# Row maxima of a 64 MB array: a short first load, the last two rows in four pieces, and merges behind them

## The chip, the cores and the metric

The kernel runs on one core of a Trainium2 chip. The metric is the device time of one execution in microseconds; lower is better. Beside it there is a profile of one execution: a page, and a trace that can be asked for timelines, waits and DMA issues.

## The reference

```python
x = np.random.randn(32, 512, 1024).astype(np.float32)

def reference(x):
    return np.max(x, axis=-1).astype(np.float32)
```

So 16384 rows of 1024 numbers are read, 67.1 MB, and one number a row is written, 64 KB.

## The kernel before, in words

The 16384 rows are spread over 128 partitions, 128 rows each. In the rest of the text "a row" means one row in every partition: 1024 elements for VectorE, 0.5 MB for the DMA engines. There are 128 of them, I in the code. `BLOCKS` cuts them into loads: a first block of 112 rows in ten loads (numbers 0 to 9, of 15, 15, 15, 14, 12, 11, 9, 8, 7 and 6 rows) and a second block of 16 rows, of which seven loads (numbers 10 to 16, of 4, 3, 2, 2, 1, 1 and 1 rows) take 14 and the last two rows come in pieces. The loads go into `ring`, a buffer of 46 rows, one behind the other; where a load does not fit any more it begins at the front again. All loads and pieces are issued by SyncE (SP), in order, L185 and L204 to L207. A load is issued when the reductions that read its place are done. SyncE's DMAs use eight semaphores in turn, so that each one also waits until the DMA eight places before it has landed.

Most of the work is on VectorE: one `reduce_max` for each load (helper `maximum`, L168), from the ring into `res`, which has one column a row. VectorE can't take all rows at the pace at which they arrive, so some columns of some rows go another way. `SHARED` names them: `9: (4, 4)` says that of load 9 the last 4 rows give their first 4 blocks of 128 columns away. `turn` (L125) transposes these blocks on TensorE into PSUM with the identity `ident` (L135), ScalarE copies them into SBUF (L141), and GpSimd (POOL) takes the maximum over the partitions (`partition_all_reduce`, L143), which is now the maximum over 128 columns of each row. `back` (L154) transposes a line of these maxima back into a column of a small PSUM tile, `fetched` (L161). VectorE reduces the other columns of these rows into the same tile, and `merge` (L170) reduces the tile over its blocks into `res`. In all 38 blocks of 128 columns go this way, in seven calls of `turn`.

The order on each engine is written out: `in_turn` chains the instructions of an engine in the order in which the program makes them. `TENSOR` lists the calls of `turn` and `back`, and `MERGE` says behind which load's reduction a merge stands.

The last two rows, seen as one line of 2048 columns in each partition, come in three pieces: the first 689 columns, the next 671, which end row one and begin row two, and the last 688. The second lies in `res` behind the place of the first one's maximum (column `AT - 1`), so that one reduction over two halves of 336 takes that maximum in, and gives both the first row's result and a maximum for the second row, at `MID - 1`, which the last reduction, of 689 columns, takes in (L212 to L217). Two merges stand between these two reductions.

The results leave by DMAs that ScalarE issues: the first block's 112 columns in three stores of 48, 48 and 32 partitions, behind the reduction of the first piece (L221), and the last 16 columns when everything is done (L223).

Of the kernel before, what the change touches and what calls it, by code (L numbers as in the profile page):

```python
# [8 lines left out]
F32 = mybir.dt.float32  # L9
# [1 line left out]


BLOCKS = [
    [15, 15, 15, 14, 12, 11, 9, 8, 7, 6],
    [4, 3, 2, 2, 1, 1, 1],
]
RING = 46


SHARED = {7: (2, 3), 9: (4, 4), 11: (3, 3), 13: (2, 3), 16: (1, 1)}  # L20


TENSOR = [
    ("turn", 7, 0), ("back", 7, 0), ("turn", 9, 0), ("turn", 9, 1),
    ("back", 9, 0), ("turn", 11, 0), ("turn", 11, 1), ("back", 9, 1),
    ("turn", 13, 0), ("back", 11, 0), ("back", 11, 1), ("turn", 16, 0),
    ("back", 13, 0), ("back", 16, 0),
]

MERGE = {8: (7,), 12: (9,), 15: (11,), 18: (13, 16)}  # L30
NOSYNC = mybir.DependencyInfo(mybir.DependencyClass.NoSync, mybir.DependencyReason.DATA)
SYNC = mybir.DependencyInfo(mybir.DependencyClass.Sync, mybir.DependencyReason.DATA)

# [1 line left out]
@with_exitstack  # L35
def kernel(
    ctx: ExitStack,
    tc: tile.TileContext,
    x: bass.AP,
    out: bass.AP,  # L40
):
    nc = tc.nc
    P = 128
    X = mybir.AxisListType.X
    ALU = mybir.AluOpType

    xf = x.flatten_outer_dims()
    N, D = xf.shape
    H = D // 2
    C = D // P  # L50
    I = N // P
    of = out.flatten_outer_dims()

    once = ctx.enter_context(tc.tile_pool(name="once", bufs=1))
    turned = ctx.enter_context(tc.tile_pool(name="turned", bufs=2))
    allr = ctx.enter_context(tc.tile_pool(name="allr", bufs=2))
    psum = ctx.enter_context(tc.tile_pool(name="psum", bufs=2, space=bass.MemoryType.PSUM))
    psmall = ctx.enter_context(tc.tile_pool(name="psmall", bufs=4, space=bass.MemoryType.PSUM))
    ring = once.tile([P, RING, D], F32)

    W = 336
    K = W - 1
    AT = I + 16
    MID = AT + K + W + 17
    res = once.tile([P, MID + D - W], F32)

    latest = {}

    def in_turn(engine, inst):

        if engine in latest:
            tc.add_manual_dep(inst.ins, latest[engine].ins.name, NOSYNC, reason="in turn")
        latest[engine] = inst
        return inst

    ident = once.tile([P, P], F32)  # L80
    colno = once.tile([P, P], F32)
    rowno = once.tile([P, 32], F32)
    in_turn("DVE", nc.vector.memset(ident, 1.0))  # L83
    in_turn("DVE", nc.vector.memset(rowno, 0.0))  # L84
    in_turn("DVE", nc.vector.tensor_tensor_scan(  # L85
        out=colno, data0=ident, data1=ident, initial=-1.0, op0=ALU.add, op1=ALU.mult))
    in_turn("DVE", nc.vector.transpose(out=rowno, in_=colno[:, :32]))  # L87
    for q in range(1, P // 32):
        part = rowno[q * 32:(q + 1) * 32, 0:1]
        in_turn("DVE", nc.vector.tensor_scalar(  # L90
            out=part, in0=part, scalar1=float(q * 32), scalar2=None, op0=ALU.add))
    in_turn("DVE", nc.vector.tensor_scalar(  # L92
        out=ident, in0=colno, scalar1=rowno[:, 0:1], scalar2=None, op0=ALU.is_equal))

    loads = []
    first = at = 0
    views = []
    for sizes in BLOCKS:
        S = sum(sizes) + 2 * (sizes is BLOCKS[-1])
        xb = xf[first * P:(first + S) * P, :].rearrange("(p i) d -> p i d", p=P)  # L100
        dst = bass.AP(tensor=of.tensor, offset=of.offset + first * P, ap=[[S, P], [1, S]])
        views.append((dst, res[:, first:first + S]))
        b = 0
        for n in sizes:
            if at + n > RING:
                at = 0
            loads.append((at, n, xb[:, b:b + n, :], first + b))
            at += n
            b += n
        first += S  # L110
    assert first == I

    def chunks(j):
        m, parts = SHARED[j]
        per = max(1, C // parts)
        return [(r, min(per, m - r)) for r in range(0, m, per)]

    def rows(j):
        start, n, _, _ = loads[j]
        return ring[:, start:start + n, :]  # L120

    tops = {}
    backs = {}

    def turn(j, c):  # L125


        m, parts = SHARED[j]
        r, q = chunks(j)[c]
        W = q * parts * P  # L130
        ps = psum.tile([P, D], F32)
        for i in range(q):
            for c0 in range(parts):
                k = i * parts + c0
                in_turn("PE", nc.tensor.transpose(  # L135
                    out=ps[:, k * P:(k + 1) * P],
                    in_=rows(j)[:, loads[j][1] - m + r + i, c0 * P:(c0 + 1) * P],
                    identity=ident,
                ))
        sb = turned.tile([P, D], F32)  # L140
        in_turn("ACT", nc.scalar.copy(out=sb[:, :W], in_=ps[:, :W]))  # L141
        top = allr.tile([P, D], F32)
        in_turn("POOL", nc.gpsimd.partition_all_reduce(  # L143
            top[:, :W], sb[:, :W], P, bass_isa.ReduceOp.max))
        tops[j, c] = top

    def share(j):
        m, parts = SHARED[j]
        if j not in backs:
            fetched = psmall.tile([P, parts + (parts < C), m], F32)  # L150
            backs[j] = fetched
        return backs[j]

    def back(j, c):  # L154

        m, parts = SHARED[j]
        r, q = chunks(j)[c]
        for i in range(q):
            for c0 in range(parts):
                k = i * parts + c0  # L160
                in_turn("PE", nc.tensor.transpose(  # L161
                    out=share(j)[:, c0, r + i:r + i + 1],
                    in_=tops[j, c][0:1, k * P:(k + 1) * P],
                    identity=ident[0:1, 0:1],
                ))

    def maximum(out, in_):
        return in_turn("DVE", nc.vector.reduce_max(out=out, in_=in_, axis=X))  # L168

    def merge(j):  # L170
        for i in MERGE.get(j, ()):
            _, k, _, c0 = loads[i]
            q, _ = SHARED[i]
            maximum(res[:, c0 + k - q:c0 + k], share(i).rearrange("p k m -> p m k"))


    issued = done = 0
    todo = list(TENSOR)
    for j in range(len(loads)):
        while issued < len(loads) and issued < j + 3:  # L180
            start, n, src, _ = loads[issued]
            held = any(s < start + n and start < s + k for s, k, _, _ in loads[j:issued])
            if held:
                break
            nc.sync.dma_start(out=rows(issued), in_=src)  # L185
            issued += 1
        while todo and todo[0][1] < (j if todo[0][0] == "back" else issued):
            what, i, c = todo.pop(0)
            (turn if what == "turn" else back)(i, c)
        _, n, _, col = loads[j]  # L190
        m, parts = SHARED.get(j, (0, 0))
        if n > m:
            maximum(res[:, col:col + n - m], rows(j)[:, :n - m, :])
        if m and parts < C:
            maximum(share(j)[:, parts, :], rows(j)[:, n - m:, parts * P:])
        merge(j)
    for what, i, c in todo:
        assert what == "back"
        back(i, c)

    if at + 1 > RING:
        at = 0
    piece = ring[:, at, :D - K]
    nc.sync.dma_start(out=piece, in_=xb[:, S - 2, :D - K])  # L204
    pair = xb[:, S - 2:, :].rearrange("p i d -> p (i d)")
    nc.sync.dma_start(out=res[:, AT:AT + K + W], in_=pair[:, D - K:D + W])
    nc.sync.dma_start(out=res[:, MID:], in_=pair[:, D + W:])  # L207
    latest_row = maximum(res[:, AT - 1:AT], piece)
    merge(len(loads))


    maximum(  # L212
        bass.AP(tensor=res.tensor, offset=res.offset + I - 2,
                ap=[list(res.ap[0]), [MID - 1 - (I - 2), 2]]),
        res[:, AT - 1:AT + K + W].rearrange("p (r k) -> p r k", r=2))
    merge(len(loads) + 1)
    maximum(res[:, I - 1:I], res[:, MID - 1:])  # L217


    for p, q in ((0, 48), (48, 96), (96, P)):  # L220
        store = nc.scalar.dma_start(out=views[0][0][p:q], in_=views[0][1][p:q])  # L221
        tc.add_manual_dep(store.ins, latest_row.ins.name, SYNC, reason="behind the loads")
    nc.scalar.dma_start(out=views[1][0], in_=views[1][1])  # L223


# [1 line left out]
_INS = ['x']  # L227
# [26 lines left out]
```

## Time and profile before

| | |
|---|---|
| time, median of 4 runs | 164.1 us (164.05 to 164.21) |
| the profiled execution | 164.21 us, of which the profile's span is 162.4 |
| VectorE (DVE) busy | 135.4 us, 83% of the span |
| TensorE (PE), ScalarE (ACT), POOL busy | 14.0, 6.4 and 16.2 us |
| DMA | 67.18 MB, mean 414 GB/s over the span |
| chain that ended last | DVE 57%, DMA 36%, issue 5% |
| `res<-ring` reductions, 15 of them | 124.1 us, idle before them 23.8, all for loads |

The span begins with the first instruction of the program and ends with its last one; the device time has 1.8 us more around it. The chain is followed back from the last instruction, at each step to what released it. In timelines a row has the start, the duration, the engine and line, the operation with output and inputs, and in brackets how long the engine was idle before and what ended that; rows marked x2 or more join instructions of one kind, and the starts and durations of neighbours can overlap a little, since VectorE begins an instruction before the one ahead of it has left its pipeline.

### The profile page before, as it was taken

To read this page: it belongs to the slowest core of one execution; us is meant where nothing else is said; L and a number is where in the kernel's file an instruction comes from. 1 tells how busy PE (TensorE), PEld (TensorE's weight loads), DVE (VectorE), ACT (ScalarE), POOL (GpSimd) and SP (SyncE) were. 2 spreads that over 40 slices of the span, in tenths; PEclk is the share of its full clock that TensorE was granted. 3 is DMA by queue.
4 is the path that set the end of the run, shared out by engine and by line. 5 is a ranking of instruction groups with operands and counts; after the bars stand their busy time and mean duration, and the time that the engine had idled before them with its cause. 6 is when DMAs were issued, how large, how long until landed. Compare 5 with 4: busy or idle time off the path is not lost.

```text
span 162.4 us, 305 instructions
## 1 busy us (share of the span) xinstructions
PE 14.0 (9%) x76; PEld 12.0 (7%) x76; DVE 135.4 (83%) x35; ACT 6.4 (4%) x8; POOL 16.2 (10%) x11
## 2 busy tenths in 40 slices
PE   0000000000000000000000000000003010736540
PEld 0000000000000000000000000000002010725440
DVE  3000069995999779998999999999999999999994
ACT  3000000000000000000000000000001000222020
POOL 0000000000000000000000000000000500095970
DMA  7998899979999799999998998999999999999990
GB/s 242 484 484 378 348 484 484 484 333 393 484 484 469 314 395 452 452 452 387 508 460 371 422 466 373 436 427 443 476 395 445 438 409 408 428 420 416 410 372 18
DMA packets 3200, 67.18 MB, mean 414 GB/s; under 512 B 640, under 2 KB 640, under 8 KB 1408
## 3 DMA queue, kind: packets, MB, share of 16 engines
q1 hardware_dynamic: 2880, 67.11, 96.7%
q10 hardware_dynamic: 320, 0.07, 0.2%
HBM read 67.11 MB, written 0.07 MB: 414 GB/s over the span
## 4 chain that ended last, share of the span: by engine, by line
DVE 57%; DMA 36%; issue 5%; DVEq 0%
DVE res L168 52%; DMA ring<-in_x_dram 36%; DVE fetched L168 5%; DVEq L249 0%
## 5 line engine op out<-in xcount | busy, mean ns | idle before, releaser
L168 DVE TENSOR_REDUCE res<-ring 128x15 f32<-128x15360 f32 (+10 forms) x15 | 124.1, 8302 | 23.8 <-DMA ring<-in_x_dram 23.8
L143 POOL PARTITION_ALL_REDUCE top<-sb x7 | 16.0, 2332 | 141.9 <-ACT sb L141 141.9
L135 PE MATMUL ps<-ident,ring 128*128 128x128 f32 x38 | 9.3, 423 | 134.0 <-DMA ring<-in_x_dram 134.0
L135 PEld LDWEIGHTS ps<-ident,ring 128*128 128x128 f32 x38 | 7.5, 222 | 134.2 <-issue 127.9
L141 ACT COPY sb<-ps 128x768 f32<-128x768 f32 (+3 forms) x7 | 5.1, 739 | 150.3 <-PE ps L135 150.3
L168 DVE TENSOR_REDUCE fetched<-ring 128x2 f32<-128x1280 f32 (+3 forms) x5 | 8.5, 1700 | 0.0
L161 PE MATMUL fetched<-ident,top 1*128 1x1 f32 x38 | 4.8, 243 | 10.8 <-DVE fetched L168 7.3
L161 PEld LDWEIGHTS fetched<-ident,top 1*128 1x128 f32 x38 | 4.5, 212 | 12.5 <-issue 8.0
L168 DVE TENSOR_REDUCE res<-res 128x2 f32<-128x672 f32 (+1 forms) x2 | 1.7, 858 | 0.0
L141 ACT ACT_TABLE_LOAD x1 | 1.3, 1283 | 0.7 <-PEq L238 0.7
L83 DVE MEMSET ident<- 128x128 f32 x1 | 0.2, 165 | 0.8 <-PEq L238 0.8
L168 DVE TENSOR_REDUCE res<-fetched 128x2 f32<-128x8 f32 (+3 forms) x5 | 0.7, 158 | 0.0
L90 DVE TENSOR_SCALAR rowno<-rowno 32x1 f32<-32x1 f32 x3 | 0.4, 146 | 0.1
L85 DVE TENSOR_TENSOR_SCAN colno<-ident 128x128 f32<-128x128 f32 x1 | 0.4, 425 | 0.0
L92 DVE TENSOR_SCALAR ident<-colno,rowno 128x128 f32<-128x128 f32 x1 | 0.3, 285 | 0.0
L87 DVE STREAM_TRANSPOSE rowno<-colno 128x32 f32<-128x32 f32 x1 | 0.2, 211 | 0.0
L238 POOL MEMSET const-float32-0.0<- 128x1 f32 x1 | 0.1, 99 | 0.2 <-issue 0.2
L238 POOL MEMSET const-bfloat16-1.0<- 128x1 bf16 x1 | 0.1, 103 | 0.0
L238 POOL MEMSET const-uint8-127<- 128x1 uint8 x1 | 0.1, 102 | 0.0
L238 POOL MEMSET const-float32-1.0<- 128x1 f32 x1 | 0.1, 99 | 0.0
L84 DVE MEMSET rowno<- 128x32 f32 x1 | 0.1, 85 | 0.0
## 6 DMA issues: line engine op xcount, KB each, us to landing
ring<-in_x_dram SPq DMA_DIRECT2D x3, 7680.0 KB, 38.5
ring<-in_x_dram SPq DMA_DIRECT2D x1, 7168.0 KB, 37.0
ring<-in_x_dram SPq DMA_DIRECT2D x1, 6144.0 KB, 33.4
ring<-in_x_dram SPq DMA_DIRECT2D x1, 5632.0 KB, 28.6
ring<-in_x_dram SPq DMA_DIRECT2D x1, 4608.0 KB, 39.1
ring<-in_x_dram SPq DMA_DIRECT2D x1, 4096.0 KB, 33.4
ring<-in_x_dram SPq DMA_DIRECT2D x1, 3584.0 KB, 29.0
ring<-in_x_dram SPq DMA_DIRECT2D x1, 3072.0 KB, 35.9
```

The source lines that it names most:

```text
L83: in_turn("DVE", nc.vector.memset(ident, 1.0))
L84: in_turn("DVE", nc.vector.memset(rowno, 0.0))
L85: in_turn("DVE", nc.vector.tensor_tensor_scan(out=colno, data0=ident, data1=ident, initial=-1.0, op0=ALU.add, op1=ALU.mult))
L87: in_turn("DVE", nc.vector.transpose(out=rowno, in_=colno[:, :32]))
L90: in_turn("DVE", nc.vector.tensor_scalar(out=part, in0=part, scalar1=float(q * 32), scalar2=None, op0=ALU.add))
L92: in_turn("DVE", nc.vector.tensor_scalar(out=ident, in0=colno, scalar1=rowno[:, 0:1], scalar2=None, op0=ALU.is_equal))
L135: in_turn("PE", nc.tensor.transpose(out=ps[:, k * P:(k + 1) * P], in_=rows(j)[:, loads[j][1] - m + r + i, c0 * P:(c0 + 1) * P], identity=i ...
L141: in_turn("ACT", nc.scalar.copy(out=sb[:, :W], in_=ps[:, :W]))
L143: in_turn("POOL", nc.gpsimd.partition_all_reduce(top[:, :W], sb[:, :W], P, bass_isa.ReduceOp.max))
L161: in_turn("PE", nc.tensor.transpose(out=share(j)[:, c0, r + i:r + i + 1], in_=tops[j, c][0:1, k * P:(k + 1) * P], identity=ident[0:1, 0:1],))
L168: return in_turn("DVE", nc.vector.reduce_max(out=out, in_=in_, axis=X))
L238: nc = _bacc.Bacc("TRN2", target_bir_lowering=False, num_devices=1)
```

## The change

The first block is cut into eleven loads, of 2, 13, 13, 15, 14, 11, 11, 10, 8, 8 and 7 rows, numbers 0 to 10; the second block's loads keep their sizes and are numbers 11 to 17. With the pieces there are 22 loads. The ring has 47 rows, and `res` is its first 128 columns instead of a tile of its own.

The shared rows are others: 3, 2 and 1 rows of loads 10, 12 and 14, six blocks each, and one row of load 17, two blocks; 38 blocks as before, in seven turns (`t0` to `t6`), one row each.

The last two rows are cut at columns 604 and 568 and come in the order 604 of row one, 568 of row two, 420 of row one, 456 of row two. A second piece lies behind one free column, into which the reduction of the same row's first piece writes its maximum; so the second reduction reads 421 or 457 columns and gives the row's result. All four reductions (`f0` to `f3`) have one input row.

The order is one list, `PLAN`: `d` is the reduction of a load's own rows, `p` that of a shared row's other columns, `t` and `b` are `turn` and `back`, `m` a merge, `f` a piece. On VectorE the tail reads: d15, d16, m12, p17, f0, f1, f2, m14, f3, m17. Loads are issued as early as the plan's readers allow. The first block's results leave in one store instead of three, behind `f0`.

```diff
 BLOCKS = [
-    [15, 15, 15, 14, 12, 11, 9, 8, 7, 6],
+    [2, 13, 13, 15, 14, 11, 11, 10, 8, 8, 7],
     [4, 3, 2, 2, 1, 1, 1],
 ]
-RING = 46
-SHARED = {7: (2, 3), 9: (4, 4), 11: (3, 3), 13: (2, 3), 16: (1, 1)}
-TENSOR = [
-    ("turn", 7, 0), ("back", 7, 0), ("turn", 9, 0), ("turn", 9, 1),
-    ("back", 9, 0), ("turn", 11, 0), ("turn", 11, 1), ("back", 9, 1),
-    ("turn", 13, 0), ("back", 11, 0), ("back", 11, 1), ("turn", 16, 0),
-    ("back", 13, 0), ("back", 16, 0),
-]
-MERGE = {8: (7,), 12: (9,), 15: (11,), 18: (13, 16)}
+RING = 47
+SHARED = {10: (3, 6), 12: (2, 6), 14: (1, 6), 17: (1, 2)}
+PIECES = [(604, 420), (568, 456)]
+PLAN = """
+    d0 d1 d2 d3 d4 d5 d6 d7 d8 d9 t0 d10 t1 t2 p10 d11 b0 b1 t3 d12 t4 p12 d13 b2 m10 t5 d14
+    p14 d15 b3 b4 d16 m12 p17 t6 f0 b5 f1 f2 b6 m14 f3 m17
+""".split()
...
-    ring = once.tile([P, RING, D], F32)
-    W = 336
-    K = W - 1
-    AT = I + 16
-    MID = AT + K + W + 17
-    res = once.tile([P, MID + D - W], F32)
+    ring = once.tile([P, I + RING * D], F32)
+    res = ring[:, :I]
...
+    at = at if at + last + 1 <= RING else 0
+    pieces = []
+    tail = []
+    room = I + at * D
+    for q in range(len(PIECES[0])):
+        for r, widths in enumerate(PIECES):
+            c, w = sum(widths[:q]), widths[q]
+            room = -(-(room + 1) // 16) * 16
+            pieces.append((ring[:, room:room + w], xb[:, S - last + r, c:c + w]))
+            if q:
+                tail[-last] = (ring[:, room - 1:room], tail[-last][1])
+            tail.append((res[:, I - last + r:I - last + r + 1],
+                         ring[:, room - (q > 0):room + w]))
+            room += w
...
-    piece = ring[:, at, :D - K]
-    nc.sync.dma_start(out=piece, in_=xb[:, S - 2, :D - K])
-    pair = xb[:, S - 2:, :].rearrange("p i d -> p (i d)")
-    nc.sync.dma_start(out=res[:, AT:AT + K + W], in_=pair[:, D - K:D + W])
-    nc.sync.dma_start(out=res[:, MID:], in_=pair[:, D + W:])
-    latest_row = maximum(res[:, AT - 1:AT], piece)
-    merge(len(loads))
-    maximum(
-        bass.AP(tensor=res.tensor, offset=res.offset + I - 2,
-                ap=[list(res.ap[0]), [MID - 1 - (I - 2), 2]]),
-        res[:, AT - 1:AT + K + W].rearrange("p (r k) -> p r k", r=2))
-    merge(len(loads) + 1)
-    maximum(res[:, I - 1:I], res[:, MID - 1:])
-    for p, q in ((0, 48), (48, 96), (96, P)):
-        store = nc.scalar.dma_start(out=views[0][0][p:q], in_=views[0][1][p:q])
-        tc.add_manual_dep(store.ins, latest_row.ins.name, SYNC, reason="behind the loads")
-    nc.scalar.dma_start(out=views[1][0], in_=views[1][1])
+    def issue():
+        nonlocal issued
+        while issued < len(loads):
+            start, n, src, _ = loads[issued]
+            if any(readers[j] and s < start + n and start < s + k
+                   for j, (s, k, _, _) in enumerate(loads[:issued])):
+                return
+            load = nc.sync.dma_start(out=rows(issued), in_=src)
+            issued += 1
+        if any(readers[j] and s < at + last + 1 and at < s + k for j, (s, k, _, _) in enumerate(loads)):
+            return
+        while pieces:
+            nc.sync.dma_start(out=pieces[0][0], in_=pieces[0][1])
+            pieces.pop(0)
+
+    for step in PLAN:
+        issue()
+        kind, k = step[0], int(step[1:])
+        if kind in "dp":
+            (direct if kind == "d" else partial)(k)
+            readers[k] -= 1
+        elif kind == "t":
+            turn(k)
+            readers[chunks[k][0]] -= 1
+        elif kind == "b":
+            back(k)
+        elif kind == "m":
+            merge(k)
+        else:
+            inst = maximum(*tail[k])
+            if behind is None:
+                behind = inst
+
+    for dst, src in views[:-1]:
+        store = nc.scalar.dma_start(out=dst, in_=src)
+        tc.add_manual_dep(store.ins, behind.ins.name, SYNC, reason="behind the loads")
+    nc.scalar.dma_start(out=views[-1][0], in_=views[-1][1])
```

## The prediction

> **What bounds the kernel now.** I read first the page's strip of 40 slices, then the chain that ended last in order of time, then VectorE's and SyncE's timelines, and last the DMA issues. The strip:
>
> ```profile
> DVE  3000069995999779998999999999999999999994
> DMA  7998899979999799999998998999999999999990
> ```
>
> Each digit is a busy tenth of 4.06 us. The DMA engines are busy from the first slice to the last but one; VectorE (DVE) has nothing to do before slice 6 and no gap from slice 19 on. Both end together, so there are two limits within a fraction of a microsecond of each other. The chain in order of time (start, length) says where VectorE hangs on a landing:
>
> ```profile
> 0.72 20.79 DMA ring<-in_x_dram
> ...
> 21.54 16.16 DVE res L168
> ...
> 74.75 55.86 DVE res L168 x5
> ```
>
> VectorE starts at 21.54, when load 0 (15 rows) has landed; from load 3 (14 rows, landed at 74.73 by the same chain) to the end it never stops. Its timeline shows the pace and the end:
>
> ```profile
> 39.67 16.15 DVE L168 TENSOR_REDUCE res<-ring 128x15 f32<-128x15360 f32 x1 [1.98 <-DMA ring<-in_x_dram]
> 57.81 16.16 DVE L168 TENSOR_REDUCE res<-ring 128x15 f32<-128x15360 f32 x1 [1.98 <-DMA ring<-in_x_dram]
> 74.75 55.86 DVE L168 TENSOR_REDUCE res<-ring 128x14 f32<-128x14336 f32 x5 [0.79 <-DMA ring<-in_x_dram]
> 130.53 1.48 DVE L168 TENSOR_REDUCE fetched<-ring 128x2 f32<-128x1280 f32 x1
> 131.92 7.61 DVE L168 TENSOR_REDUCE res<-ring 128x7 f32<-128x7168 f32 x1
> 139.45 0.16 DVE L168 TENSOR_REDUCE res<-fetched 128x2 f32<-128x8 f32 x1
> ...
> 157.46 0.86 DVE L168 TENSOR_REDUCE res<-ring 128x1 f32<-128x689 f32 x1
> 158.36 0.85 DVE L168 TENSOR_REDUCE res<-res 128x2 f32<-128x672 f32 x1
> 159.13 0.22 DVE L168 TENSOR_REDUCE res<-fetched 128x2 f32<-128x8 f32 x2
> 159.27 0.86 DVE L168 TENSOR_REDUCE res<-res 128x1 f32<-128x689 f32 x1
> ```
>
> From start to start, five reductions of 52 rows take 130.53 - 74.75 = 55.78 us and one of 7 rows takes 7.53. Two equations give 1.0665 us a row and 0.065 an instruction. The last reduction ends at 160.13.
>
> The stream's pace is in SyncE's timeline, whose late issues wait for the landing of the load eight places before (they take over its semaphore):
>
> ```profile
> 131.75 0.33 SPq L185 DMA_DIRECT2D ring<-in_x_dram  x1
> 139.06 0.33 SPq L204 DMA_DIRECT2D ring<-in_x_dram  x1
> 143.95 0.33 SPq L206 DMA_DIRECT2D res<-in_x_dram  x1
> 147.64 0.33 SPq L207 DMA_DIRECT2D res<-in_x_dram  x1
> ```
>
> Of the DMA issues (KB, us from issue to landing) I use two:
>
> ```profile
> res<-in_x_dram SPq DMA_DIRECT2D x1, 344.0 KB, 11.4
> out_dram<-res ACTq DMA_DIRECT2D x1, 8.0 KB, 1.4
> ```
>
> SyncE's rows are the landings of loads 8, 9, 10 and 11 (7, 6, 4 and 3 rows): 7.31 us for 6 rows, 4.89 for 4, 3.69 for 3. With 16.94 for 14 rows (57.81 to 74.75) and 18.14 for 15 (39.67 to 57.81), all lie on 1.205 us a row plus 0.07 a load. What is left of load 0 is the start: 21.51 - 18.14 = 3.37. The formula 3.37 + 1.205 x rows + 0.07 x loads puts load 9 at 139.03 (seen: just before 139.06) and the last of 20 loads at 159.01 (seen: 147.64 + 11.4 = 159.04).
>
> **The sum, against the profiled execution.** It took 164.21 us for a span of 162.4, and the median of the runs is 164.1; I compute the end of VectorE's work against 160.13 and put the difference on the median. What comes behind (the final store issued at 160.16, landed 1.4 later, end at 162.4) does not change.
>
> Stream after: the same 128 rows, 22 loads instead of 20. Load 4 (57 rows in) lands at 3.37 + 68.69 + 0.35 = 72.41; load 7 (89 rows) at 111.18; load 9 (105 rows) at 130.60; load 10 (112 rows) at 139.10; the last piece at 3.37 + 154.24 + 1.54 = 159.15, so 0.14 later than the formula gives before. The queue does not run dry: load 4 waits for reduction 1 (over at about 35.5) while load 3 lands at 55.46; load 6 waits for reduction 3 (71.6) while load 5 lands at 85.7; the last piece waits for load 13 (150.2), nine microseconds of stream ahead of it.
>
> Here a rule speaks against more and smaller loads. The Trainium skill, "DMA: Bandwidth & Descriptors", section "Anatomy of one DMA", fits about 2.0 us fixed for a DMA beside its bytes (on the GpSimd path). Were that paid in line, two more loads would cost 4 us and the time would be 168; the landings above show 0.07 a load as long as another one is queued.
>
> VectorE after: the first reduction (2 rows, 2.2 us from 5.87) lies in the time in which it idles now. Reductions 1 to 4 each wait for their load, since a row takes 1.07 us and lands in 1.21. It idles 3.4 us before load 0, 13.5 before load 1, 1.8 before load 2, 4.2 before load 3 and 0.9 before load 4, 23.8 together, where it now idles 19.0, 2.0, 2.0 and 0.8 before loads 0 to 3, 23.8: the early start is given back at the loads after it. What counts is the last wait. Reduction 4 starts at 72.43; 36 rows in three instructions take 38.59, to 111.02; load 7 is there at 111.18, so reduction 7 starts at 111.20 and ends at 121.93, reduction 8 at 130.53; load 9 is there at 130.60, reduction 9 starts at 130.62 and ends at 139.22, just behind load 10. From there it is not held again: 14 whole rows (14336 elements), parts of 768, 512, 256 and 768, pieces of 604, 568, 421 and 457, three merges of 42 elements come to 18732 elements, 19.51 us, and 18 instructions to 1.17. The last merge (148 ns, as the shortest of now) starts at 159.90 and ends at 160.05. The rows of before show that small instructions cost somewhat more (0.14 instead of 0.08 for one merge), for which I allow 0.1: 160.05 to 160.15, against 160.13. The last reduction (457 elements) would begin at 159.36, 0.2 after its piece.
>
> The two late reductions of 672 and 689 columns go: the row at 157.46 took 0.90 to the next start where the pace gives 0.78, because the next one waits for its result in the same engine. After, a second piece's reduction reads a maximum that is two or three instructions old, so 0.12 goes; two more instructions bring 0.13. VectorE's elements stay: 38 blocks of 128 columns leave for TensorE before and after.
>
> TensorE's route is squeezed: now one of seven all-reduces is over by 128.3; after, all come behind load 10. POOL and TensorE today:
>
> ```profile
> 152.72 1.51 PE L135 MATMUL ps<-ident,ring 128*128 128x128 f32 x6 [1.87 <-DMA ring<-in_x_dram]
> 155.22 3.19 POOL L143 PARTITION_ALL_REDUCE top<-sb  x2 [1.06 <-ACT sb L141]
> ```
>
> From TensorE's start to POOL's is 2.50, from a landing to TensorE's start some 0.13. An all-reduce of 768 columns takes 2.50 (the single one at 125.80), one of 256 about 1.05 (between 0.69 for 128 and 1.41 for 384, both differences of such pairs). So t0 to t2 run 141.73 to 149.23, t3 (load 12 at 147.68) from 150.31, t4 to 155.31, t5 to 157.81, t6 to 158.86. Six transposes back take 0.77 (at 132.16). Merge m12 needs t4's, there at 156.2, and is due at 156.49; m14 has 158.7 against 159.29; m17 has 159.2 against 159.90. All are hidden, m12 by 0.3 us; if that cover is gone, VectorE waits for the difference and the end moves with it.
>
> The store in one piece instead of three is issued behind f0, near 158.3; three issues hold ScalarE until 159.7 today, one shorter, and the final store waits for VectorE either way. Its transfer (1.5 us from issue to landing in each of today's three) ends near the last piece's landing, in which VectorE has 0.2 to spare: nothing. The steps where results and ring become one tile add no wait to any queue.
>
> Sum: VectorE's end changes by -0.08 to +0.02, that is, nothing: 164.1.
>
> **Rivals.** (1) Faster: the start shortens with a smaller first load. The first load takes 2.65 us more than a load in the stream (20.79 - 18.14), while the final store goes from issue to landing in 1.4. If the 1.25 between them belongs to the size of the first load, every landing comes earlier, and the end, hung on loads 4 and 9, moves with them: 0 to -1.25, middle -0.6, 163.5. Against it: the same engines start on the same queue. (2) Slower: landings without a reserve. VectorE waits for loads 7 and 9, at their landing, so what any of the first ten loads is late is late at the end, one for one; today it has a reserve from load 4 on (by the formula load 4 lands at 89.28 and is wanted at 89.75, and later ones have more). It passes 0.2% when load 9 lands 0.35 later than computed: 0.105 a load instead of 0.07, or a bubble behind the 2-row load. From 0 to one more start, 2.65; nearest to the rows is 0.4 to 0.7, 164.6. For it: the rows say nothing of a short load at the start. Against it: short loads in the tail land at the pace. (3) Slower: the squeezed route. If all-reduces take 0.15 longer each, or PE comes late, m12 waits, from 0.3 of slip on; 0.5 more slip gives 164.6. Against it: today's all-reduces run beside VectorE as well and pairs of them take no more than their sum.
>
> **How the numbers follow.** About 0.2% (0.33 us) is what a measurement here tells from no change. Forecast within it: 0.57, own range 163.8 to 164.4. Rival 1: 0.17. Rival 2: 0.18. Rival 3: 0.08. So faster 0.17, same 0.57, slower 0.26. The range leaves out the far half of rival 1 and the far part of 2 and 3: 163.6 to 164.8.
>
> **What would show it.** Right: reduction 4 starts near 72.4 and VectorE is then idle only for a tenth or two, at loads 7 and 9; the last merge ends near 160.1; the last piece lands near 159.15. Wrong by rival 1: load 0 lands clearly before 5.85, load 1 before 21.58. Wrong by rival 2: waits of over 0.3 at reductions 7, 9 or 10, with load 9 past 130.9. Wrong by rival 3: idle time before m10, m12 or m14 that ends with a transpose back. A last reduction that waits for its piece would mean that the stream sets the end.

## The result, and the profile after

The changed kernel takes 163.87 us (median of 33 runs, 163.73 to 164.02) against 164.07 (53 runs, 163.87 to 164.49): 0.9987 of the time before, interval 0.9982 to 0.9992. That is 0.20 us less: small, but the interval does not reach 1. The profiled execution took 163.84 us for a span of 162.1.

The page's strip of 40 slices still has both limits busy to the end:

```profile
DVE  3500079978996399989999999999999999999994
DMA  5999999997999869999898999799999999999991
```

VectorE's timeline of the changed kernel, first its waits for loads, then its end:

```profile
5.62 2.29 DVE L74 TENSOR_REDUCE ring<-ring 128x2 f32<-128x2048 f32 x1 [3.11 <-DMA ring<-in_x_dram]
21.33 14.02 DVE L74 TENSOR_REDUCE ring<-ring 128x13 f32<-128x13312 f32 x1 [13.43 <-DMA ring<-in_x_dram]
37.07 14.02 DVE L74 TENSOR_REDUCE ring<-ring 128x13 f32<-128x13312 f32 x1 [1.72 <-DMA ring<-in_x_dram]
55.21 16.15 DVE L74 TENSOR_REDUCE ring<-ring 128x15 f32<-128x15360 f32 x1 [4.12 <-DMA ring<-in_x_dram]
72.15 71.23 DVE L74 TENSOR_REDUCE ring<-ring 128x14 f32<-128x14336 f32 x7 [0.79 <-DMA ring<-in_x_dram]
...
157.16 1.94 DVE L74 TENSOR_REDUCE ring<-ring 128x1 f32<-128x604 f32 x3
159.02 0.16 DVE L74 TENSOR_REDUCE ring<-got 128x1 f32<-128x7 f32 x1
159.09 0.62 DVE L74 TENSOR_REDUCE ring<-ring 128x1 f32<-128x457 f32 x1
159.63 0.15 DVE L74 TENSOR_REDUCE ring<-got 128x1 f32<-128x3 f32 x1
```

The shape is the one that was computed: the idle time is spread over five loads, and the last merge ends it. The row of 71.23 joins seven reductions and hides two short waits. The chain that ended last shows them:

```profile
71.77 39.14 DMA ring<-in_x_dram
110.91 0.02 issue
110.94 19.41 DVE ring L74 x2
130.35 0.02 issue
130.37 13.01 DVE ring L74 x2
```

Load 7 lands at 110.91 and load 9 at 130.34, and each reduction starts 0.03 later; by the prediction's pace VectorE waits 0.2 us for the first and 0.1 for the second. So the last wait is at load 9, as computed (0.18 and 0.09). But every row is early. The first reduction starts at 5.62 and not 5.87, the one of 14 rows at 72.15 and not 72.43, and the end is 159.78 and not 160.05 to 160.15. SyncE's late issues (each waits for a landing eight places before) say the same of the stream, loads 9 and 10 landed just before 130.41 and 138.87, some 0.2 ahead of the sum:

```profile
130.41 0.33 SPq L209 DMA_DIRECT2D ring<-in_x_dram  x1
138.87 11.41 SPq L214 DMA_DIRECT2D ring<-in_x_dram  x4
```

Nothing in between went faster than computed: from the reduction of 14 rows to the end of VectorE it is 159.78 - 72.15 = 87.63 us, where the sum had 160.05 - 72.43 = 87.62. What moved against the sum is the start of the stream.

One remark on the description of the kernel before, which says that VectorE can't take all rows at the pace at which they arrive. The rows measured there say otherwise: 1.07 us a row against a landing every 1.205. What holds VectorE back is that it gets the rows a whole load at a time, the first 15 only at 21.54.

VectorE's list of waits (us, times, longest; the two short waits above are not in it) has no TensorE and no POOL:

```profile
DVE ring L74 <- DMA ring<-in_x_dram: 23.2, 5, 13.4
DVE ident L79 <- PEq L252: 0.8, 1, 0.8
```

The squeezed route is hidden, as the timeline of POOL and TensorE shows:

```profile
141.38 7.48 POOL L146 PARTITION_ALL_REDUCE top<-sb  x3 [140.96 <-ACT sb L144]
...
150.19 8.52 POOL L146 PARTITION_ALL_REDUCE top<-sb  x4 [1.32 <-ACT sb L144]
...
155.23 0.79 PE L156 MATMUL got<-ident,top 1*128 1x1 f32 x6 [0.43 <-POOL top L146]
```

The last row is `b4`: over at 156.02, and merge m12 starts at 156.19. The cover was 0.3 by the sum and is 0.2.

### The profile page after: what moved, and what is told of

Read it like the earlier page. It is cut to its first block, busy times and chain, and to the rows that moved or that the text cites. A ratio compares the mean times of both kernels' runs of the same rounds, so it can differ in the third digit from the quotient of the medians.

```text
span 162.1 us, 306 instructions
## 1 busy us (share of the span) xinstructions
PE 13.6 (8%) x76; PEld 11.8 (7%) x76; DVE 135.5 (84%) x37; ACT 6.5 (4%) x8; POOL 16.2 (10%) x11
## 4 chain that ended last, share of the span: by engine, by line
DVE 48%; DMA 46%; another core or an unknown queue 3%; SPq 1%; issue 0%; DVEq 0%
DVE ring L74 47%; DMA ring<-in_x_dram 46%; DVE got L74 1%; SPq L209 1%; DVEq L263 0%
## 5 line engine op out<-in xcount | busy, mean ns | idle before, releaser
L74 DVE TENSOR_REDUCE ring<-ring 128x1 f32<-128x1024 f32 (+12 forms) x21 | 131.5, 6293 | 23.3 <-DMA ring<-in_x_dram 23.2
L144 ACT COPY sb<-ps 128x768 f32<-128x768 f32 (+1 forms) x7 | 5.2, 738 | 150.3 <-PE ps L138 149.0
L156 PE MATMUL got<-ident,top 1*128 1x1 f32 x38 | 4.8, 236 | 4.4 <-POOL top L146 2.9
L156 PEld LDWEIGHTS got<-ident,top 1*128 1x128 f32 x38 | 4.3, 199 | 6.0 <-POOL top L146 5.3
L74 DVE TENSOR_REDUCE got<-ring 128x3 f32<-128x768 f32 (+3 forms) x4 | 3.0, 753 | 0.0
L74 DVE TENSOR_REDUCE ring<-got 128x3 f32<-128x21 f32 (+3 forms) x4 | 0.6, 160 | 0.0
```

The lines of the kernel that those rows point to most:

```text
L156: in_turn("PE", nc.tensor.transpose(out=share(j)[:, c, r + i:r + i + 1], in_=tops[k][0:1, w:w + P], identity=ident[0:1, 0:1],))
```

## The experiments

Three theories stood at first. Theory 1: the start, every landing comes earlier since the first load is short. Theory 2: the tail, in which no reduction waits for its neighbour's result. Theory 3: VectorE's early two rows. Each group of runs shares one chip and the runs of the kernel before on it.

**First load of 15 rows in the changed kernel** (the numbers in `SHARED` and `PLAN` follow):

```diff
-    [2, 13, 13, 15, 14, 11, 11, 10, 8, 8, 7],
+    [15, 13, 15, 14, 11, 11, 10, 8, 8, 7],
```

> The changed kernel with its first two loads (2 and 13 rows) joined into one of 15; all else is its own. Theory 1 (the start: short first packets bring the DMA engines into step sooner, and every landing comes earlier): load 0 lands at about 21.5 as before the change, the load of 14 rows lands 0.2 later than in the changed kernel, and the time rises by about 0.2 us over the changed kernel, to 164.05. Theory 2 (the gain is in the tail: no reduction waits for its neighbour's result, pieces in another order): nothing is lost, one load fewer saves 0.07, so 163.8. Theory 3 (VectorE's early two rows bring the gain): VectorE starts 2.3 us of work later, but waits for the same landings afterwards; a gain lost of up to 0.2, with landings that do not move.

164.06 us, 0.9995 of before (0.9986 to 1.0004). Most of the gain is gone, although there is one load fewer and the tail is the changed one: theory 2 is not enough. (About 0.07 of the loss lies behind VectorE's end and has nothing to do with the first load, as shown below.)

**The first load of the kernel before cut into 2 and 13**, all else its own:

```diff
-    [15, 15, 15, 14, 12, 11, 9, 8, 7, 6],
+    [2, 13, 15, 15, 14, 12, 11, 9, 8, 7, 6],
```

> The kernel before with its first load of 15 rows cut into 2 and 13; tail, shares and ring are its own. Theory 1: the load of 14 rows lands some 0.2 earlier in spite of one more load, and the time falls by about 0.2 us, to 163.87, as far as the changed kernel. Theory 2: one more load costs 0.07, no gain: 164.1 to 164.2. Theory 3: VectorE has its two rows early, but the stretch to the end still starts at the load of 14 rows; 164.1, with landings that do not move.

163.81 against 164.12 on this chip, 0.9982 (0.9973 to 0.9991). The timeline shows where:

```profile
5.35 2.29 DVE L168 TENSOR_REDUCE res<-ring 128x2 f32<-128x2048 f32 x1 [2.84 <-DMA ring<-in_x_dram]
...
74.35 55.86 DVE L168 TENSOR_REDUCE res<-ring 128x14 f32<-128x14336 f32 x5 [0.80 <-DMA ring<-in_x_dram]
```

The reduction of 14 rows starts 0.40 earlier than the 74.75 of before, in spite of one more load, and the profiled execution took 163.82, 0.39 less than the 164.21 of before. (The execution of before that was profiled was a slow one; between the medians it is 0.31.) Theory 3 would have left the landings where they were.

**A first load of 1 row** in the changed kernel (1 and 14 instead of 2 and 13):

> The changed kernel with a first load of 1 row and a second of 14 instead of 2 and 13. Theory 1, if the first packet's length is what counts (4 KB instead of 8): the spread of the engines shrinks further or stays, and the time is 163.75 to 163.87. If it is the whole first load that hides the spread, half of the gain is gone: 163.95. Theories 2 and 3: 163.87, no change.

163.63 (163.56 to 163.76), 0.9969 (0.9956 to 0.9981), 0.12 under the lower end of theory 1's range. The row of 14 in VectorE's timeline is 0.18 earlier than in the changed kernel:

```profile
71.97 71.21 DVE L74 TENSOR_REDUCE ring<-ring 128x14 f32<-128x14336 f32 x7 [0.79 <-DMA ring<-in_x_dram]
```

It did not hold on other chips, as shown below.

**A short DMA ahead of the loads of the kernel before**:

```diff
+    early = once.tile([P, P], F32)
+    nc.sync.dma_start(out=early, in_=xf[:P, :P])
```

> The kernel before with one more DMA ahead of all loads, which brings the first 128 columns (512 bytes) of 128 rows into a tile that nobody reads. Theory 1: short packets come first, so the engines are in step earlier; the load of 15 rows lands earlier by up to 0.2, less the 0.1 that a further DMA costs: 163.95 to 164.1. If it is the load's size and not its first packets, or theory 2 or 3: it costs its own 0.1, and the time is 164.15 to 164.2.

164.74, 1.0036 (1.0023 to 1.0048), 0.5 over the highest that any theory had. VectorE's timeline has the first load of 15 rows 0.40 later than without it (21.94 against 21.54), and the load of 14 rows 0.43 later:

```profile
21.94 16.15 DVE L171 TENSOR_REDUCE res<-ring 128x15 f32<-128x15360 f32 x1 [19.43 <-DMA ring<-in_x_dram]
...
75.18 55.87 DVE L171 TENSOR_REDUCE res<-ring 128x14 f32<-128x14336 f32 x5 [0.79 <-DMA ring<-in_x_dram]
```

By the trace the short DMA's packets run from 1.76 to 2.47 us. The next load is issued 0.42 later than it is without the short DMA, and its packets begin at 2.22 instead of 1.72. So this first DMA was too short to cover the start of the next one. It is the bubble of the prediction's rival 2, made by hand, and it goes to the end in full: the two profiled executions differ by 0.46.

**First loads of 4 and of 8 rows** in the changed kernel (4 and 11, 8 and 7):

> The changed kernel with a first load of 4 rows and a second of 11, instead of 2 and 13. So far the time was 164.06 with a first load of 15 rows, 163.87 with 2 and 163.63 with 1. Theory 1a (what the first packet of each DMA engine loses grows with its length, 16 KB here): between 15 and 2 rows, 163.9 to 164.0. Theory 1b (only very short first packets gain, and 2 rows gain because of what follows them): 164.06.

164.00, 0.9995 (0.9986 to 1.0003).

> The changed kernel with a first load of 8 rows and a second of 7. Theory 1a: 164.0 to 164.1, near the 164.06 of a first load of 15 rows. Theory 1b: 164.06 as well, and the same as with 4 rows. If 8 rows are as fast as 2, the length of the first packet doesn't count.

163.87, 0.9987 (0.9978 to 0.9996), as fast as with 2 rows and faster than with 4. "What the first packet loses grows with its length" falls: the times don't follow the size.

**The first load of the kernel before cut into 1 and 14**:

> The kernel before with its first load of 15 rows cut into 1 and 14; its tail, three stores and ring are its own. If the start is all of the gain, it goes with the tail of the kernel before as well: one load fewer than the changed kernel with a first load of 1 row (163.63), so 163.55 to 163.65, and 0.2 less than the same kernel cut into 2 and 13 (163.81). If the changed tail brings part of the gain, it stays above 163.7.

164.09, 1.0004 (0.9995 to 1.0012). Nothing of the 0.5 that 1 row had gained with the changed tail on the other chip.

**The four pieces by row**, so that a second reduction reads its neighbour's result:

```diff
-    for q in range(len(PIECES[0])):
-        for r, widths in enumerate(PIECES):
+    for r, widths in enumerate(PIECES):
+        for q in range(len(widths)):
...
-                tail[-last] = (ring[:, room - 1:room], tail[-last][1])
+                tail[-1] = (ring[:, room - 1:room], tail[-1][1])
```

> The changed kernel with the four pieces by row: 604 and 420 of row one, then 568 and 456 of row two, so that the second reduction reads what the one just ahead of it wrote. If such a wait costs 0.12, as the row at 157.46 of the kernel before says, the last reduction starts 0.1 later and the time is 163.97. If the order of pieces brings nothing, 163.87.

163.98, 0.11 over the changed kernel. Its timeline:

```profile
157.12 2.05 DVE L74 TENSOR_REDUCE ring<-ring 128x1 f32<-128x604 f32 x3
159.09 0.15 DVE L74 TENSOR_REDUCE ring<-got 128x1 f32<-128x7 f32 x1
159.21 0.63 DVE L74 TENSOR_REDUCE ring<-ring 128x1 f32<-128x457 f32 x1
```

The three reductions take 2.05 instead of 1.94: 0.11 for the one result that is read at once, where the prediction had 0.12 for such a wait. The last one, which reads a result with a merge in between, starts 2.09 behind the first instead of 1.93, so it loses 0.05 more.

**Programs that differ off the path.** The times for 1 row on two chips (163.63 and 164.09) left two readings: the program as a whole sets the start (theory B), or first loads do and the third load matters too (theory A). Four kernels change only the first block's store, one for three or three for one:

```diff
-    for dst, src in views[:-1]:
-        store = nc.scalar.dma_start(out=dst, in_=src)
+    dst, src = views[0]
+    for p, q in ((0, 48), (48, 96), (96, P)):
+        store = nc.scalar.dma_start(out=dst[p:q], in_=src[p:q])
```

> The kernel before with its first block's results in one store instead of three; its first load of 15 rows stays. The store is off the path, so by the prediction's step 164.1. Theory A (the first loads' sizes set the start): the start stays with them, so 164.1. Theory B (the start differs from program to program by up to 0.3, whatever its first load): anything from 163.8 to 164.4, though the store itself costs nothing.

164.16, 1.0004 (0.9995 to 1.0013), not told from the kernel before; the trace shows 0.11 more behind VectorE's end, as told below.

> The changed kernel with a first load of 15 rows and with three stores instead of one. With one store it took 164.06. Theory A: 164.06. Theory B: 163.75 to 164.35, and its first landing moves with the time.

163.94, 0.9993 (0.9984 to 1.0002).

> The changed kernel with a first load of 1 row and three stores instead of one. With one store it took 163.63. Theory A: 163.63. Theory B: up to 0.3 more, 163.6 to 163.95.

164.12 (163.81 to 164.28), 1.0001 (0.9992 to 1.0010), where the same first loads with one store had given 163.63.

> The kernel before with a first load of 1 row, a second of 14, and one store instead of three. With three stores it took 164.09. Theory A: 164.09. Theory B: 163.7 to 164.3, and its first landing moves with the time.

164.20, 1.0004 (0.9995 to 1.0013).

The runs had been on different chips, so that a third reading stood (theory C): the chip decides. The next group puts the same programs on one:

> The changed kernel itself once more, beside its neighbours on one chip. Theory A (first loads' sizes): 163.87. Theory B (program): 163.87, since the program is the same. Theory C (the chip decides how the engines start): may differ by up to 0.3 from 163.87.

163.86, 0.9989 (0.9980 to 0.9998).

> The changed kernel with a first load of 1 row, 163.63 on another chip. Theory A: at or under 163.87 as there. Theory B: 163.63 again, and 0.4 less than the same kernel with three stores. Theory C: as that one with three stores, both 163.6 or both 164.1.

163.96, 0.9994 (0.9986 to 1.0003).

> The changed kernel with a first load of 1 row and three stores, 164.12 on another chip. Theory B: 164.12 again. Theories A and C: the same as with one store, within 0.1.

164.00, 0.9993 (0.9984 to 1.0001).

> The changed kernel with a first load of 15 rows, 164.06 on another chip and 163.94 on a third with three stores. Theory A: 0.1 to 0.2 more than the changed kernel beside it. Theories B: 164.06. Theory C: anything within 0.3 of it, moving with the others.

163.98, 0.9995 (0.9986 to 1.0004).

The row of 14 of the kernel with a first load of 1 row on this chip, and then that of the one with 15:

```profile
72.20 71.30 DVE L74 TENSOR_REDUCE ring<-ring 128x14 f32<-128x14336 f32 x7 [0.79 <-DMA ring<-in_x_dram]
```

```profile
72.22 71.23 DVE L73 TENSOR_REDUCE ring<-ring 128x14 f32<-128x14336 f32 x7 [0.79 <-DMA ring<-in_x_dram]
```

The first was at 71.97 on the other chip. With 1 row, one store and three differ by 0.04 here, so the 0.49 between them on two chips was not the program's (theory B). The very kernel that took 163.63 on one chip takes 163.96 on this one, while the kernel before takes 164.06 to 164.12 on all of them: with a first load of 1 row, the chip or the occasion decides as much as the change. The changed kernel itself repeats, 163.87 and 163.86, and is 0.12 below the first load of 15 rows beside it, for which two causes are found below. One group remained, on a further chip:

> The kernel before with its first load cut into 2 and 13, which gained 0.31 on one chip, where the same kind of kernel with 1 row did well too. If the first load's size sets the start on every chip: 0.2 to 0.3 under the kernel before again. If that was this chip's: between 0 and 0.1 under it, one more load being paid for.

164.00, 0.9993 (0.9984 to 1.0002): 0.10 under the kernel before, at the edge of the second expectation, where it was 0.31 on the first chip. Its runs spread from 163.70 to 164.18.

> The changed kernel with first loads of 8 and 7 rows, 163.87 on one chip, as fast as with 2 and 13. If size counts, it lies between 163.87 and the 163.98 to 164.06 of a first load of 15 rows; if the chip decides, anything within 0.2 of these.

163.81, 0.9983 (0.9974 to 0.9992): 8 rows are as good as 2 again, on another chip.

**One number that orders all of them.** In every kernel VectorE waits for a load of 14 rows and has no wait over 0.2 us behind it. Its start (the row `128x14` with a wait for the DMA in VectorE's timeline) beside the time of the same execution:

| kernel | median us | profiled us | 14 rows start | difference |
|---|---|---|---|---|
| before, first load 15 | 164.07 | 164.21 | 74.75 | 89.46 |
| before, 2 and 13 | 163.81 | 163.82 | 74.35 | 89.47 |
| the same, another chip | 164.00 | 163.79 | 74.31 | 89.48 |
| before, 1 and 14 | 164.09 | 164.20 | 74.72 | 89.48 |
| before, short DMA ahead | 164.74 | 164.67 | 75.18 | 89.49 |
| changed, 2 and 13 | 163.87 | 163.84 | 72.15 | 91.69 |
| the same, another chip | 163.86 | 163.74 | 72.09 | 91.65 |
| changed, 15 | 164.06 | 163.88 | 72.13 | 91.75 |
| the same, another chip | 163.98 | 163.98 | 72.22 | 91.76 |
| changed, 8 and 7 | 163.87 | 163.95 | 72.26 | 91.69 |
| changed, 4 and 11 | 164.00 | 163.98 | 72.33 | 91.65 |
| changed, 1 and 14 | 163.63 | 163.63 | 71.97 | 91.66 |
| the same, another chip | 163.96 | 163.96 | 72.20 | 91.76 |

(The kernels with other stores lie within 0.1 of these; the one with pieces by row has 91.88.) Within each tail the difference is constant to 0.03 or 0.11 us while the times differ by 0.9 and 0.35. So the time is the landing of that load plus a nearly fixed rest, and as the stream's pace is the same in all of them, the landing is set by the start of the stream. The rest falls by a tenth with the change: 57 rows in five loads should land 2 x 1.205 - 0.07 = 2.34 before 59 rows in four, and the rest grew by 91.69 - 89.46 = 2.23 only, so plan and tail bring 0.11.

**What the rest hides.** It has two parts. From the reduction of 14 rows to VectorE's end it is 85.36 to 85.38 in all seven profiles with the tail of before, and 87.59 to 87.63 in those with the changed tail (87.70 once, where load 9 kept VectorE longer, and 87.80 with the pieces by row). Behind VectorE's end it is not constant. The last rows of the changed kernel and of the one with 15 rows, side by side on one chip:

```profile
159.54 0.15 DVE L74 TENSOR_REDUCE ring<-got 128x1 f32<-128x3 f32 x1
```

```profile
159.68 0.15 DVE L73 TENSOR_REDUCE ring<-got 128x1 f32<-128x3 f32 x1
```

From there to 163.74 and 163.98 it is 4.05 and 4.15. Over all 20 profiles this part goes with the number of DMAs that the program issues: 4.04 to 4.08 with 24 of them (nine profiles), 4.10 to 4.15 with 23 or 25 (eight), 4.18 and 4.19 with 22 or 26 (three). At the program's end SyncE waits for the eight semaphores in a fixed order. With 24 DMAs the last store has the one that is asked last. With 23, in the kernel with 15 rows, SyncE has the last store's at 161.29 and asks for one more, 0.06 later. This is 0.06 of the 0.10 between the two; the other 0.04 stays open.

So of the 0.12 between the changed kernel and the one with 15 rows on this chip, 0.10 lies behind VectorE's end. Taking VectorE's part and the part behind it off the medians gives an estimate of the landing of the 14 rows: 72.21 with 2 rows and 72.22 with 15. The changed kernel has one load more ahead of it, 0.07 by the formula, so its start is some 0.08 shorter. The same estimate for the kernel before cut into 2 and 13 has the landing 0.32 and 0.11 earlier than without the cut (74.34 against 74.66 on one chip, 74.53 against 74.64 on the other).

**Where the start is lost.** In every profile the first packet of the stream begins between 1.71 and 1.76. But the first packets run long: in the kernel before up to 3275 ns, where the same packets later take 2267, and in the changed kernel up to 1271 where later ones take 309. Added up over the first load and divided by the 16 DMA engines, what its packets take above their shortest is 0.78 us in the kernel before, and 0.48 and 0.44 when it is cut into 2 and 13. With the changed tail it is 0.51 to 0.67 for 2 rows and 0.62 to 0.71 for 15. With 1 row it is 0.37 in the execution that has the 14 rows at 71.97, and 0.61 in the one of the same program that has them at 72.20. So much of what moves the start is in these packets. What slows them no run shows.

## Why the prediction was wrong

**The stream's pace** (1.205 a row, 0.07 a load) held: between loads 0 and 10 of the changed kernel, 110 rows and ten loads, it gives 133.25; from 5.59 to 138.85 in the trace it was 133.26. So no bubble stood behind the 2-row load, and rival 2 did not come: load 9 landed at 130.34, and not past 130.9. **VectorE's chain** from the load of 14 rows held too: 87.62 computed, 87.63 measured. **The squeezed route** waited nowhere, so rival 3 did not come, though m12's cover shrank to 0.2. **The neighbour's result** costs 0.12 by the sum, and 0.11 was measured by putting it back. **The single store** changes nothing before VectorE's end; the number of DMAs, 24 before and after, happens to leave what is behind it as it was (4.08 and 4.06), which the prediction did not look at.

Two terms were off. The smaller one is the allowance of 0.1 for small instructions: it was not needed. Without it the sum had VectorE's end 0.08 earlier, and at an equal start the traces show 0.09 (85.38 to 87.63, 2.25, against 2.34). The prediction called this nothing.

**The step that failed is the start**, "What is left of load 0 is the start: 21.51 - 18.14 = 3.37", carried over unchanged to the changed kernel. Load 0 of the changed kernel landed at 5.59, which leaves 5.59 - 2.48 = 3.11. In the two profiled executions that is 0.26 of the 0.37 between 164.21 and 163.84; the other 0.11 is the rest above. Two things are in the 0.26. The execution that was profiled before was 0.14 above the median of 164.07, and the one after 0.03 under its own; since the rest is nearly constant, it is their starts that stood apart by these 0.17, and taking one execution's start for the start was the first mistake. What then remains is 0.09 of the 0.20 between the medians (the other 0.11 being 0.09 of VectorE's chain and 0.02 behind it, which is within the scatter there). This 0.09 is an estimate by subtraction. That it comes from the first load is supported by the kernel before, where nothing else was changed and the cut into 2 and 13 gained 0.31 on one chip and 0.10, at the edge of the noise, on another.

So rival 1 was right in its sign, and its sign of being wrong came (load 0 at 5.59 and not 5.85, load 1 at 21.31 and not 21.58, though 0.17 of each is the chance of the two executions). It was far off in its size: the prediction gave it 0 to 1.25 with a middle of 0.6, and on one chip it came to between nothing and 0.3, the further load paid for. Its mechanism, that the 1.25 belongs to the size of the first load, is not what the runs show: 8 rows do as well as 2, 4 rows do not, and 1 row gains 0.5 on one chip and 0.1 or nothing on others. The measured 163.87 lies in the range of 163.8 to 164.4, but at its edge and for a reason that the forecast did not have. The forecast of no change within 0.33 us missed a gain of 0.20; that bound was too wide as well, for the measured interval reaches only 0.05% to either side.

What is not settled is why the first load moves the start: the loss is seen in its packets, and what slows these stays open. Differences of 0.1 to 0.3 remain between chips for the same program with short first loads. The chip as the cause is argued from the same program on two chips, with nothing else tried. No version was found that beats the changed kernel on more than one chip: 8 and 7 rows (163.87 and 163.81) can't be told from it.

## What to carry to other kernels

Where the bounding engine hangs on a landing and the stream never pauses, a change at the first DMA moves the end one for one (the short DMA ahead: 0.43 at the load of 14 rows, 0.46 at the end): treat the start as a term of its own, with a spread of its own. Take such a term from several executions and not from the one profiled; here one execution's start was 0.14 us off, more than half of the effect that was sought. And when effects of 0.1% are in question, compare kernels on the same chip, and look for a quantity inside the trace (here a landing and the rest behind it) that splits the time in a part that varies and one that does not. Check the part that is held to be fixed as well: here a tenth of a microsecond behind the last reduction went with the number of DMAs, and 0.10 of the 0.12 between two kernels would have been credited to the first load.

## What the runs showed of the hardware

- The 16 completion signals of the first load of 15 rows came between 20.79 and 21.51 in the kernel before, 0.72 apart, and those of its last piece between 158.44 and 159.08, 0.64 apart. In the changed kernel it was 0.36 apart at the first load and 0.35 at the last. So the distance between the first signal and the last, which VectorE waits for (21.51, and its reduction at 21.54), hardly changes from the first load to the last piece. In the five profiles with a first load of 2 rows this spread was 0.30 to 0.42, in all others 0.46 to 0.80.
- The 0.07 us of a load fit a cost of its packets. By the trace a load is 128 packets, eight for each of 16 engines if they share evenly; one of 61440 bytes takes 2267 ns and one of 4096 bytes 160. Both lie on 150.5 ns for 4096 bytes and some 10 ns a packet, eight of which make 0.08.
- Executions of one program on one chip differ by up to 0.6 us (163.87 to 164.45 for the kernel before). Where one program was profiled twice, most of the difference was in the start: 72.15 and 72.09 for 163.84 and 163.74, 71.97 and 72.20 for 163.63 and 163.96.
